# Scores of stick-breaking attention: the keys' low parts kept in 64 rows per head instead of 128

## The chip, the cores and the metric

The kernel runs on one core of a Trainium2 chip. The metric is the device time of one execution in microseconds (us), as a median of several runs. All engine times come from one execution that the hardware profiler recorded. The engines are named as the profile names them: PE (TensorE matmul), PEld (TensorE weight load), DVE (VectorE), ACT (ScalarE), POOL (GpSimd), SP (the queue that issues most DMAs).

## What is computed

One decoder layer over 1024 positions and 1024 channels in float32: a norm, one input projection, a gated short convolution beside eight heads of attention, an output projection, an MLP, a gate, a norm. The change lies in the attention. For each head of 64 channels the reference computes

```python
z = einsum('bhqd,bhkd->bhqk', q, k) * scale          # scores, 64 channels
mask = key_pos[None, :] < q_pos[:, None]
log_keep = where(mask, log_sigmoid(-z), 0.0)
suffix = cumsum(log_keep, axis=3, reverse=True) - log_keep
a = where(mask, exp(log_sigmoid(z) + suffix), 0.0)
out = einsum('bhqk,bhkd->bhqd', a, v)
```

## The kernel before

Every large product takes float32 operands apart into a high part, rounded to the matmul's format, and a low part, the rest. In the projections three matmuls are summed: high x high, high x low, low x high. ACT makes a high part (a copy), DVE the low part (a subtraction).

The scores use the fact that a head has 64 channels and a matmul sums over 128 rows. The query tile of a head holds the high parts in the 64 rows that the head owns (rows 0 to 63 for head 0 of a pair, 64 to 127 for head 1) and the low parts in the other 64. For the keys there are two tiles per head: K1 holds the high parts in both halves, K2 the low parts in both halves. Two matmuls over 128 rows then give the sum of all four products (L583).

The heads come in four pairs. `qk_projection(pr)` makes the queries and keys of a pair: for each half of the positions (512), 24 matmuls (L155) fill one bank of PSUM, ACT copies the high parts out of it (L449, L463, L464), and DVE subtracts (L450, L465, L466). L465 writes the low parts of the keys into the head's own rows, L466 into the other 64. The tiles come from a group of nine units ("QK"); a projection waits until six are free and takes two for the queries and four for the keys. A head's three units go back when its last score is issued.

`attend_front` computes scores for blocks of 128 queries: per piece of up to 512 keys one pair of matmuls (L583), two sigmoids on ACT (L585, L586), a mask on POOL (L590), running products on DVE (L593, L598), a product on POOL or DVE (L600). There are 96 such pieces. `back_transposes` turns 128x128 blocks of the result on PE (L612), ACT rounds them (L617), DVE takes the low parts (L618). `back_values` multiplies by the values (L642): the high part first, then the low part, so its second matmul waits for L618. ACT and DVE add up the halves (L650, L651). `head_norm` (L483 to L498, with a power on POOL at L494) runs in between.

On PE the order is the program's own. `attention_slots` yields slots, and between the slots the generator `fillers` hands out matmuls of the projections, the convolution branch and the output projection, 8 per slot. Between two scores PE therefore has other matmuls to do. In this stage the order on ACT, DVE, POOL and SP is set by a scheduler at build time, and each engine takes its queue strictly in that order. The stage runs from about 100 us to 454 us of the span; the MLP follows.

Of the kernel before, what the change touches and what calls it, by code (L numbers as in the profile page):

```python
# [10 lines left out]
F32R = mybir.dt.float32r  # L11
AF = mybir.ActivationFunctionType
ALU = mybir.AluOpType

P = 128
# [41 lines left out]
def f32(ap):  # L57
    return ap.bitcast(F32)
# [3 lines left out]
def hybrid_layer_kernel(ctx: ExitStack, tc: tile.TileContext, x, p, g_mix, w_in, conv_w, g_conv_out,  # L62
                        g_attn_out, w_out, g_mlp, w_up, w_down, g_ple, w_ple_gate, w_ple_proj,
                        g_final, out):
    nc = tc.nc
    x, p, w_in, conv_w, w_out, w_up, w_down, w_gate, w_proj, out = (
        x[0], p[0, 0], w_in[0], conv_w[0], w_out[0], w_up[0], w_down[0], w_ple_gate[0], w_ple_proj[0], out[0])
# [6 lines left out]
    U = Units(upool, {"A": 16, "VY": 10, "QK": 9, "T": 9, "W": 5, "C": 2, "E": 3})  # L74
    PS_BUFS = {"mm": 2, "z": 2, "tr": 2, "av": 2}

    def bank(tag):
        return psum.tile([P, HB], F32, name="ps_" + tag, tag=tag, bufs=PS_BUFS[tag])
# [309 lines left out]
    def proj_bank(ps, w2, h):  # L388
        yield from product_steps(ps, [(w2[0][0][:, d, :], w2[1][0][:, d, :], aT(h, d, 0), aT(h, d, 1))
                                      for d in range(KT)])  # L390

    class Stream:
# [17 lines left out]
        def next(self):  # L410
            self._split()
            return self.ready.popleft()
# [17 lines left out]
    QK = {}  # L430
# [1 line left out]
    normed = set()  # L432

    def qk_projection(pr):
        while len(U.free_q["QK"]) < 6:
            yield 0
        w2 = stream.next()
        Q = [U.get("QK", F32R) for _ in range(2)]
        K = [[U.get("QK", F32R) for _ in range(2)] for _ in range(2)]
        QK[pr] = (Q, K)  # L440
        for h in range(NH):
            ps = bank("mm")
            yield from proj_bank(ps, w2, h)
            sl = slice(h * HB, (h + 1) * HB)
            for hd in range(2):
                src = ps[hd * 64:hd * 64 + 64]
                hi = Q[hd][0][hd * 64:hd * 64 + 64, sl]
                lo = Q[hd][0][64 - hd * 64:128 - hd * 64, sl]
                nc.scalar.activation(hi, src, AF.Copy, scale=0.125)  # L449
                nc.vector.scalar_tensor_tensor(out=lo, in0=src, scalar=0.125, in1=f32(hi),  # L450
                                               op0=ALU.mult, op1=ALU.subtract)
        stream.done(w2)
        w2 = stream.next()
        for h in range(NH):
            ps = bank("mm")
            yield from proj_bank(ps, w2, h)
            sl = slice(h * HB, (h + 1) * HB)
            for hd in range(2):
                src = ps[hd * 64:hd * 64 + 64]
                own = slice(hd * 64, hd * 64 + 64)  # L460
                oth = slice(64 - hd * 64, 128 - hd * 64)
                K1, K2 = K[hd][0][0], K[hd][1][0]
                nc.scalar.copy(out=K1[own, sl], in_=src)  # L463
                nc.scalar.copy(out=K1[oth, sl], in_=src)  # L464
                nc.vector.tensor_tensor(out=K2[own, sl], in0=src, in1=f32(K1[own, sl]), op=ALU.subtract)  # L465
                nc.vector.tensor_tensor(out=K2[oth, sl], in0=src, in1=f32(K1[own, sl]), op=ALU.subtract)  # L466
        stream.done(w2)
        qk_ready.add(pr)

# [91 lines left out]
    def attend_front(pr, hd, c):  # L561
        Q, K = QK[pr]
        q, k1, k2 = Q[hd][0], K[hd][0][0], K[hd][1][0]
        both = c < 2
        if both:
            ku, bu = U.get("T", F32), U.get("T", F32)
        views, units = [], []
        for i, tb in enumerate((2 * c, 2 * c + 1)):
            n = P * (tb + 1)
            if both:  # L570
                keep, beta = ku[0][:, i * HB:i * HB + n], bu[0][:, i * HB:i * HB + n]
            else:
                ku, bu = U.get("T", F32), U.get("T", F32)
                keep, beta = ku[0][:, 0:n], bu[0][:, 0:n]
            views.append(beta)
            if i == 1 or not both:
                units.append(bu)
            cut = 384 if n == 640 else HB
            for s0 in ((cut, 0) if n > HB else (0,)):
                s1 = n if s0 or n <= HB else cut  # L580
                z = bank("z")
                for j, k in enumerate((k1, k2)):
                    nc.tensor.matmul(z[:, :s1 - s0], q[:, tb * P:(tb + 1) * P], k[:, s0:s1],  # L583
                                     start=(j == 0), stop=(j == 1))
                nc.scalar.activation(keep[:, s0:s1], z[:, :s1 - s0], AF.Sigmoid, scale=-1.0)  # L585
                nc.scalar.activation(beta[:, s0:s1], z[:, :s1 - s0], AF.Sigmoid)  # L586
                e = s1
                if s1 == n:
                    dg = beta[:, n - P:n]
                    nc.gpsimd.affine_select(out=dg, in_=dg, pattern=[[-1, P]], compare_op=ALU.is_gt, fill=0.0,  # L590
                                            base=0, channel_multiplier=1)
                    rev = keep[:, n - P:n][:, ::-1]
                    nc.vector.tensor_tensor_scan(out=rev, data0=rev, data1=future[:, ::-1], initial=1.0,  # L593
                                                 op0=ALU.mult, op1=ALU.max)
                    s1, e = n - P, n - 1
                if s1 > s0:
                    rev = keep[:, s0:s1][:, ::-1]
                    nc.vector.tensor_tensor_scan(out=rev, data0=rev, data1=rev, initial=keep[:, s1:s1 + 1],  # L598
                                                 op0=ALU.mult, op1=ALU.bypass)
                (nc.vector if s0 > 0 and pr < 3 else nc.gpsimd).tensor_tensor(  # L600
                    out=beta[:, s0:e], in0=beta[:, s0:e], in1=keep[:, s0 + 1:e + 1], op=ALU.mult)
                if s0 == 0 and (i == 1 or not both):
                    U.put(ku)
                yield views, units

    def back_transposes(ch, jp, narrow):
        c, views = ch["c"], ch["views"]
        tp = bank("tr")
        diag = jp == c
        blocks = [(2 * jp, 0), (2 * jp, 1)] + ([] if diag else [(2 * jp + 1, 0)]) + [(2 * jp + 1, 1)]  # L610
        for i, (j, t) in enumerate(blocks):
            nc.tensor.transpose(tp[:, i * P:(i + 1) * P], views[t][:, j * P:(j + 1) * P], ident)  # L612
            next(narrow, None)
        w = len(blocks) * P
        aT2 = U.get("T", F32R, (P, 2, HB))
        ah, al = aT2[0][:, 0, :], aT2[0][:, 1, :]
        nc.scalar.copy(out=ah[:, :w], in_=tp[:, :w])  # L617
        nc.vector.tensor_tensor(out=al[:, :w], in0=tp[:, :w], in1=f32(ah[:, :w]), op=ALU.subtract)  # L618
        if diag:
            for u in ch["units"]:  # L620
                U.put(u)
        return aT2
# [39 lines left out]
    def attention_slots():  # L662

        def fronts():
            for pr in range(4):
                while pr not in qk_ready:
                    yield -1
                for hd in range(2):  # L670
                    for c in range(4):
                        ch = {"pr": pr, "hd": hd, "c": c}
                        for views, units in attend_front(pr, hd, c):
                            ch["views"], ch["units"] = views, units
                            yield pr
                        for jp in range(c + 1):
                            backq.append((slot[0] + LAG, ch, jp))
                    Q, K = QK[pr]
                    U.put(Q[hd])
                    for u in K[hd]:  # L680
                        U.put(u)

        fr = fronts()
        live = True
        while live or backq or pend:
            slot[0] += 1
            narrow = iter(())
            while pend and pend[0][0] <= slot[0]:
                for _ in narrow:
                    pass  # L690
                narrow = back_values(*pend.popleft()[1:])
                next(narrow, None)
            if backq and backq[0][0] <= slot[0]:
                _, ch, jp = backq.popleft()
                pend.append((slot[0] + LAG_V, ch, jp, back_transposes(ch, jp, narrow)))
            for _ in narrow:
                pass
            run_deferred()
            if live and len(U.free_q["T"]) >= 3:
                live = next(fr, None) is not None  # L700
            yield
# [948 lines left out]
```

## Time and profile before

| | us |
|---|---|
| median of 3 runs (1270.54 to 1271.71) | 1270.54 |
| the profiled execution | 1272.67 |
| its span, first to last instruction | 1271.0 |
| PE busy | 1213.7 (95%) |
| DVE busy | 975.7 (77%) |
| ACT busy | 628.2 (49%) |
| POOL busy | 232.2 (18%) |

Matmuls overlap in the records: a record of 512 columns lasts about 0.4 us, while the starts lie 0.23 us apart in an undisturbed row. A busy share of 100% therefore means that PE never lacks work; what one matmul costs is read from the distances of the starts. The view of waits names the engine for which an idle engine waited. Over the whole span TensorE's granted clock was 0.987 of full speed.

### The profile page before, as it was taken

How to read it: one execution, taken by the hardware profiler on the slowest of the kernel's cores; microseconds unless marked ns; L12 is line 12 of the kernel's file. 1: busy time of each engine (PE TensorE's matmuls, PEld its weight loads, DVE VectorE, ACT ScalarE, POOL GpSimd, SP SyncE). 2: the span in 40 equal slices, each digit the busy share in tenths (PEclk: the TensorE clock that was granted, in tenths of full speed). 3: DMA queues.
4: the chain of work that ended last, by engine and by line, in shares of the span. 5: the costliest groups of instructions: out<-in, count | busy, mean ns of one | idle time of the engine just before them, and what ended most of it. 6: DMA issues, size and time to landing. Idle time of an engine off the chain costs nothing.

```text
span 1271.0 us, 15672 instructions
## 1 busy us (share of the span) xinstructions
PE 1213.7 (95%) x5629; PEld 1002.6 (79%) x5629; DVE 975.7 (77%) x1422; ACT 628.2 (49%) x1049; POOL 232.2 (18%) x248
## 2 busy tenths in 40 slices
PE   8999999999998899899999999987999999999997
PEld 6788878878877688678888888865788888887786
DVE  3656898999989986777666766656889888877774
ACT  4445465555656442456555555462344444445543
POOL 2402443535448540100000000000000000002121
PEclk8999999999999999999999999998999999999999
DMA  9711101111122315324577677789887886667432
GB/s 360 220 34 41 36 25 34 34 34 34 34 67 83 116 51 201 113 91 156 203 282 260 245 283 259 266 287 322 256 258 230 255 260 200 203 202 226 138 100 100
DMA packets 152229, 209.71 MB, mean 165 GB/s; under 512 B 8004, under 2 KB 111448, under 8 KB 152152
## 3 DMA queue, kind: packets, MB, share of 16 engines
q1 hardware_dynamic: 151608, 207.67, 48.7%
q8 instruction: 44, 0.72, 0.2%
q10 hardware_dynamic: 544, 1.05, 0.2%
q14 instruction: 33, 0.27, 0.1%
HBM read 141.58 MB, written 67.11 MB: 164 GB/s over the span
## 4 chain that ended last, share of the span: by engine, by line
PE 50%; DMA 4%; DVE 4%; ACT 1%; issue 1%; SPq 0%; POOL 0%; DVEq 0%; POOLq 0%; ACTq 0%
PE ps_z L1013 12%; PE ps_mm L1013 12%; PE ps_av L1013 12%; PE ps_tr L1013 7%; DMA u<-h_d 2%; PE ps_z L155 2%; PE ps_tr L155 2%; PE ps_mm L155 2%; PE ps_av L155 2%; DVE u L905 1%; DVE u L1276 1%; DVE u L836 1%; DMA n_d<-u 1%; DMA u<-hs_d 1%; DVE u L839 1%
## 5 line engine op out<-in xcount | busy, mean ns | idle before, releaser
L155 PE MATMUL ps_mm<-u,u 128*128 128x512 f32 (+1 forms) x1464 | 366.5, 396 | 7.7 <-ACT u L901 2.8
L155 PEld LDWEIGHTS ps_mm<-u,u 128*128 128x128 f32 x1464 | 270.1, 190 | 62.6 <-ACT u L901 3.2
L905 DVE TENSOR_TENSOR u<-u,u 128x1024 fp32r<-128x1024 f32 (+2 forms) x214 | 231.0, 1099 | 42.4 <-ACT u L901 35.2
L901 ACT CAST u<-u 128x1024 fp32r<-128x1024 f32 (+2 forms) x214 | 195.1, 952 | 90.4 <-DVE u L839 20.4
L1013 PE MATMUL ps_z<-u,u 128*128 128x512 f32 x768 | 195.9, 398 | 14.0 <-DVE u L905 6.7
L1013 PE MATMUL ps_mm<-u,u 128*128 128x512 f32 x768 | 191.9, 392 | 5.0 <-DVE u L836 4.4
L1013 PE MATMUL ps_av<-u,u 128*128 128x512 f32 x744 | 185.6, 391 | 2.0 <-DVE u L905 1.4
L1013 PEld LDWEIGHTS ps_z<-u,u 128*128 128x128 f32 x768 | 146.5, 192 | 47.9 <-DVE u L905 8.3
L1013 PEld LDWEIGHTS ps_mm<-u,u 128*128 128x128 f32 x768 | 145.2, 189 | 36.6 <-DVE u L836 5.3
L1013 PEld LDWEIGHTS ps_av<-u,u 128*128 128x128 f32 x744 | 140.0, 188 | 32.6 <-DVE u L905 2.1
L120 POOL TENSOR_SCALAR me<-ms 128x1 f32<-128x1 f32 x24 | 10.3, 431 | 704.7 <-DVE u L836 618.0
L836 DVE TENSOR_TENSOR u<-ps_av,u 128x512 f32<-128x512 f32 x94 | 64.6, 688 | 80.6 <-PE ps_av L1013 47.7
L1013 PE MATMUL ps_tr<-u,u 128*128 128x512 f32 x408 | 100.4, 389 | 0.0
L600 POOL TENSOR_TENSOR u<-u,u 128x383 f32<-128x383 f32 (+5 forms) x72 | 72.5, 1009 | 110.5 <-DVE u L598 70.9
L1013 PEld LDWEIGHTS ps_tr<-u,u 128*128 128x128 f32 x408 | 76.5, 188 | 15.9
L839 DVE TENSOR_TENSOR u<-u,u 128x512 f32<-128x512 f32 (+1 forms) x120 | 84.2, 723 | 1.7
L598 DVE TENSOR_TENSOR_SCAN u<-u 128x128 f32<-128x128 f32 (+3 forms) x88 | 83.7, 951 | 2.3 <-ACT u L585 0.3
L617 ACT CAST u<-ps_tr 128x512 fp32r<-128x512 f32 (+1 forms) x80 | 43.4, 543 | 58.3 <-PE ps_tr L612 57.7
L642 PEld LDWEIGHTS ps_av<-u,u 128*128 128x128 f32 x320 | 50.1, 189 | 24.7 <-DVE u L618 17.9
L642 PE MATMUL ps_av<-u,u 128*128 128x256 f32 (+1 forms) x320 | 54.8, 284 | 13.6 <-DVE u L618 13.2
L110 ACT CAST u<-u 128x1024 fp32r<-128x1024 f32 x42 | 43.9, 1055 | 29.1 <-DVE u L498 10.4
L494 POOL TENSOR_TENSOR hrs<-hms,mhalf 128x16 f32<-128x16 f32 x16 | 52.7, 3296 | 28.8 <-DVE hms L492 28.7
(132 smaller groups left out, 1502.7 us busy)
## 6 DMA issues: line engine op xcount, KB each, us to landing
u<-in_w_down SPq DMA_DIRECT2D x56, 512.0 KB, 5.4
u<-hs_d SPq DMA_DIRECT2D x64, 448.0 KB, 5.8
hs_d<-u SPq DMA_DIRECT2D x48, 512.0 KB, 2.8
u<-in_w_up SPq DMA_DIRECT2D x32, 512.0 KB, 6.0
ws_d<-u SPq DMA_DIRECT2D x32, 512.0 KB, 2.8
u<-ws_d SPq DMA_DIRECT2D x32, 512.0 KB, 6.4
u<-in_w_in SPq DMA_DIRECT2D x24, 512.0 KB, 4.2
u<-in_x SPq DMA_DIRECT2D x16, 512.0 KB, 8.1
```

The costliest lines, as they stand in the source:

```text
L110: nc.scalar.copy(out=hi, in_=raw)
L155: nc.tensor.matmul(ps, a, b, start=(i == 0), stop=(i == n - 1))
L494: nc.gpsimd.tensor_tensor(out=rs, in0=ms, in1=mhalf, op=ALU.pow)
L598: nc.vector.tensor_tensor_scan(out=rev, data0=rev, data1=rev, initial=keep[:, s1:s1 + 1], op0=ALU.mult, op1=ALU.bypass)
L600: (nc.vector if s0 > 0 and pr < 3 else nc.gpsimd).tensor_tensor(out=beta[:, s0:e], in0=beta[:, s0:e], in1=keep[:, s0 + 1:e + 1], op=ALU.mult)
L617: nc.scalar.copy(out=ah[:, :w], in_=tp[:, :w])
L642: nc.tensor.matmul(av[:, t0:256], v, part[:, c0:c0 + 256 - t0], start=(j == 0 and part is ah), stop=(j == n - 1 and part is al))
L836: (eng or nc.vector).tensor_tensor(out=out, in0=a, in1=b, op=ALU.add)
L839: (eng or nc.vector).tensor_tensor(out=out, in0=a, in1=b, op=ALU.subtract)
L901: nc.scalar.copy(out=box["o"][0], in_=src())
L905: nc.vector.tensor_tensor(out=b, in0=src(), in1=f32(a), op=ALU.subtract)
L1013: nc.tensor.matmul(ps, a, b, start=(fresh and i == 0), stop=(i == n - 1), skip_group_check=not fresh)
```

## The change

The low parts of the keys are written once, into the head's own 64 rows. So both heads of a pair share one unit for them, and L466 goes away: 16 subtractions of 64x512, in each of the four pairs one per head and half. The second matmul of a score now takes 64 rows of the query tile, the high parts, and the 64 rows of low key parts. The product of low and low is no longer in the sum. A projection of queries and keys takes five units instead of six.

```diff
 def qk_projection(pr):
-    while len(U.free_q["QK"]) < 6:
+    while len(U.free_q["QK"]) < 5:
         yield 0
     w2 = stream.next()
     Q = [U.get("QK", F32R) for _ in range(2)]
-    K = [[U.get("QK", F32R) for _ in range(2)] for _ in range(2)]
+    KL = U.get("QK", F32R)
+    K = [[U.get("QK", F32R), KL] for _ in range(2)]
...
             nc.scalar.copy(out=K1[own, sl], in_=src)
             nc.scalar.copy(out=K1[oth, sl], in_=src)
             nc.vector.tensor_tensor(out=K2[own, sl], in0=src, in1=f32(K1[own, sl]), op=ALU.subtract)
-            nc.vector.tensor_tensor(out=K2[oth, sl], in0=src, in1=f32(K1[own, sl]), op=ALU.subtract)
...
             z = bank("z")
-            for j, k in enumerate((k1, k2)):
-                nc.tensor.matmul(z[:, :s1 - s0], q[:, tb * P:(tb + 1) * P], k[:, s0:s1],
-                                 start=(j == 0), stop=(j == 1))
+            own = slice(hd * 64, hd * 64 + 64)
+            nc.tensor.matmul(z[:, :s1 - s0], q[:, tb * P:(tb + 1) * P], k1[:, s0:s1], start=True, stop=False)
+            nc.tensor.matmul(z[:, :s1 - s0], q[own, tb * P:(tb + 1) * P], k2[own, s0:s1], start=False, stop=True)
...
         U.put(Q[hd])
-        for u in K[hd]:
-            U.put(u)
+        U.put(K[hd][0])
+        if hd == 1:
+            U.put(K[hd][1])
```

The scheduler gives ACT, DVE, POOL and SP a slightly other order. On DVE, in the projection of the third pair (in the trace about 267 to 275 us), the rows before are these. The names are tiles; the number behind u_ tells units apart; order prints the running products of L598 as SCALAR_TENSOR_TENSOR.

```order
L465 TENSOR_TENSOR u_2273<-ps_mm,u_2272 64x512
L600 TENSOR_TENSOR u_2526<-u_2526,u_2525 128x511
L466 TENSOR_TENSOR u_2273<-ps_mm,u_2272 64x512
L618 TENSOR_TENSOR u_2547<-ps_tr,u_2547 128x512
L465 TENSOR_TENSOR u_2275<-ps_mm,u_2274 64x512
L466 TENSOR_TENSOR u_2275<-ps_mm,u_2274 64x512
L497 STREAM_TRANSPOSE u_2485<-hrs 128x512
L618 TENSOR_TENSOR u_2577<-ps_tr,u_2577 128x384
L598 SCALAR_TENSOR_TENSOR u_2525<-u_2525 128x512
L498 SCALAR_TENSOR_TENSOR u_1962<-u_1962,gc,u_2485 128x512
```

The same place on DVE in the changed kernel, where the subtraction of L465 stands in line 466:

```order
L466 TENSOR_TENSOR u_2262<-ps_mm,u_2263 64x512
L600 TENSOR_TENSOR u_2515<-u_2515,u_2514 128x511
L618 TENSOR_TENSOR u_2536<-ps_tr,u_2536 128x512
L466 TENSOR_TENSOR u_2262<-ps_mm,u_2264 64x512
L618 TENSOR_TENSOR u_2564<-ps_tr,u_2564 128x384
L598 SCALAR_TENSOR_TENSOR u_2514<-u_2514 128x512
L497 STREAM_TRANSPOSE u_2474<-hrs 128x512
L498 SCALAR_TENSOR_TENSOR u_1952<-u_1952,gc,u_2474 128x512
```

Both copies of L466 are gone, and the transposition of L497 has moved behind the second L618 and the running product of L598. The projection of the fourth pair changes in the same way.

On PE nothing moves; every matmul stands where it stood. Around a score of the first pair the rows before are these (u_824 and u_825 are K1 and K2 of head 0, u_822 its queries, L155 a projection that fills in):

```order
L155 MATMUL ps_mm<-u_211,u_886 128x512
L155 MATMUL ps_mm<-u_215,u_886 128x512
L155 MATMUL ps_mm<-u_211,u_887 128x512
L583 MATMUL ps_z<-u_824,u_822 128x256
L583 MATMUL ps_z<-u_825,u_822 128x256
L155 MATMUL ps_mm<-u_211,u_886 128x512
```

And in the changed kernel (u_825 is now K1, u_824 the shared tile of low parts):

```order
L155 MATMUL ps_mm<-u_211,u_885 128x512
L155 MATMUL ps_mm<-u_215,u_885 128x512
L155 MATMUL ps_mm<-u_211,u_886 128x512
L583 MATMUL ps_z<-u_825,u_822 128x256
L584 MATMUL ps_z<-u_824,u_822 128x256
L155 MATMUL ps_mm<-u_211,u_885 128x512
```

Only the second matmul of the score differs: it has its own line, and it reads 64 rows where its neighbours on both sides read 128.

## Rows read from the trace of the kernel before

**Rows 1.** Stretches, scores of L583 alone: length, PE busy (matmuls), PEld busy (loads), clock, DMA.

```profile
100.00:116.40 16.40, 1.85 (x8) 1.50 (x8) 1.00 0.22 65
116.40:181.30 64.90, 11.02 (x38) 5.84 (x38) 1.00 0.11 33
181.30:274.20 92.90, 14.55 (x50) 7.69 (x50) 1.00 0.10 29
274.20:359.00 84.80, 13.99 (x48) 7.28 (x48) 1.00 0.14 44
359.00:401.20 42.20, 7.59 (x28) 4.20 (x28) 1.00 0.17 57
401.20:454.00 52.80, 6.44 (x22) 3.08 (x21) 0.97 0.32 111
```

**Rows 2.** PE's waits, first four stretches (us, times, longest); the fifth reads as the second.

```profile
PE ps_mm L155 <- DVE u L466: 0.4, 1, 0.4
...
PE ps_av L642 <- DVE u L618: 1.7, 1, 1.7
...
PE ps_av L642 <- DVE u L618: 2.7, 3, 1.2
...
PE ps_av L642 <- DVE u L618: 2.6, 3, 1.2
```

**Rows 3.** The last stretch, all work: PE, PEld, DVE, ACT, POOL busy.

```profile
401.20:454.00 52.80, 45.65 (x226) 36.33 (x226) 52.03 (x78) 26.34 (x49) 33.26 (x28) 0.97 0.32 111
```

**Rows 4.** DVE by line, the whole span: count, busy us, mean ns, idle before.

```profile
L466 DVE TENSOR_TENSOR u<-ps_mm,u 64x512 fp32r<-64x512 f32 x16 | 11.0, 689 | 0.2
```

**Rows 5.** Timeline of DVE in the third pair's projection: start, us, instruction.

```profile
268.82 0.69 DVE L466 TENSOR_TENSOR u<-ps_mm,u 64x512 fp32r<-64x512 f32 x1
269.54 0.69 DVE L618 TENSOR_TENSOR u<-ps_tr,u 128x512 fp32r<-128x512 f32 x1
...
271.46 0.69 DVE L466 TENSOR_TENSOR u<-ps_mm,u 64x512 fp32r<-64x512 f32 x1
272.18 0.71 DVE L497 STREAM_TRANSPOSE u<-hrs 128x512 f32<-128x512 f32 x1
272.92 0.56 DVE L618 TENSOR_TENSOR u<-ps_tr,u 128x384 fp32r<-128x384 f32 x1
```

**Rows 6.** Timeline of ACT at that place, with its idle time and whom it awaited.

```profile
269.54 0.58 ACT L463 CAST u<-ps_mm 64x512 fp32r<-64x512 f32 x1 [3.69 <-DVE u L466]
```

**Rows 7.** Timeline of PE at that place.

```profile
270.29 0.62 PE L642 MATMUL ps_av<-u,u 128*128 128x256 f32 x3 [1.19 <-DVE u L618]
...
273.54 0.56 PE L642 MATMUL ps_av<-u,u 128*128 128x256 f32 x3 [1.14 <-DVE u L618]
```

**Rows 8.** Timeline of PE, and of its weight loads, around L105, which has 20 rows.

```profile
24.06 0.84 PE L155 MATMUL ps_mm<-u,u 128*128 128x512 f32 x3
24.84 0.23 PE L105 MATMUL ps_tr<-ident,u 20*128 20x20 f32 x1
25.00 0.38 PE L135 MATMUL ps_tr<-ident,u 128*128 128x128 f32 x1
...
25.45 1.30 PE L155 MATMUL ps_mm<-u,u 128*128 128x512 f32 x5
...
24.83 0.13 PEld L105 LDWEIGHTS ps_tr<-ident,u 20*128 20x128 f32 x1 [0.35 <-issue]
```

**Rows 9.** Timeline of PE where nothing disturbs it, with a score.

```profile
302.18 2.23 PE L155 MATMUL ps_mm<-u,u 128*128 128x512 f32 x9
304.25 0.60 PE L612 MATMUL ps_tr<-ident,u 128*128 128x128 f32 x4
304.60 0.71 PE L583 MATMUL ps_z<-u,u 128*128 128x512 f32 x2
305.15 0.40 PE L155 MATMUL ps_mm<-u,u 128*128 128x512 f32 x1
```

## The prediction, made before the changed kernel ran

> **What bounds the kernel now.** I read the page's busy shares first, then the waits of PE and the busy time in the attention stage (100 to 454 us), because both edits lie there, and last the timelines at the two places where they act. PE leads them and DVE follows, so a microsecond counts if it is PE's own work or a wait of PE. The stage holds 96 score pairs, 192 matmuls. I cut it where PE waits, into six stretches; by the counts of [rows 1] they hold 4, 19, 25, 24, 14 and 10 pairs (the pair at 401 us touches two stretches and is counted in the fifth). In the first five PE waits 0.4, 1.7, 2.7, 2.6 and 1.7 us for DVE [rows 2], 9.1 us together: nearly always the second value matmul (L642), which needs the low part from L618. In the last stretch DVE is busy 52.03 of 52.80 us and PE 45.65 [rows 3]; there DVE sets the time, and PE has some 7 us to spare. So PE has little slack in the stage and DVE, beside it, hardly more.
>
> **What the change removes.** L466 goes: 16 subtractions of 689 ns, 11.0 us of DVE [rows 4]. Most of it is off the path, since DVE idles or catches up elsewhere. It counts where PE waits behind it:
> - First stretch: PE waits 0.4 us for an L466 itself [rows 2], since the subtraction is the last reader of the projection's bank. That wait ends.
> - Third pair's projection: L618 at 269.54 stands right behind an L466 at 268.82 [rows 5], and PE's wait of 1.19 us ends with it [rows 7]. Without L466 it starts 0.7 us sooner. The next wait, 1.14 us, is for the L618 at 272.92, which stands behind another L466 and behind L497; the changed order puts L497 after it. ACT's copy for head 1 at 269.54 had idled 3.69 us for an L466 [rows 6]; it too starts earlier. This second wait can vanish. Together 0.7 + 1.14 = 1.8 us.
> - Fourth pair's projection: the same pattern, waits of the same size (three, longest 1.2, sum 2.6) [rows 2], so another 1.8 us.
> - Second pair's projection and the fifth stretch: the waits of 1.7 us stand before the second pair's L466 and well after the fourth pair's last ones. No gain.
>
> Sum of the gain, if nothing else changed: 0.4 + 1.8 + 1.8 = 4.0 us. The unit saved changes no wait: five units are free at the same moment as six were, when head 0 of the pair before is done. On PE no instruction moves. On SP one load of x goes ahead of two loads of w_out, which come long before their use; on ACT and POOL a few neighbours swap. I cost these at nothing, because none of them ends a wait in [rows 2]; if one did, it would be by one instruction, well under 1 us.
>
> **What the change adds.** The second matmul of a pair runs as many columns as before, so it streams no faster, and weight loads are already hidden: nine matmuls of 512 columns start within 304.25 - 302.18 = 2.07 us, 0.23 us each [rows 9]. A gain on PE is therefore excluded. What is new is that each of the 96 pairs goes from 128 rows to 64 and back. The trace has one instruction over fewer rows, the 20-row transposition of L105. Three matmuls from 24.06 should have let it start 0.69 us later; it started 0.78 us later, at 24.84 [rows 8]: 0.09 us late, and its weight load, idle before, waited for nothing that the profile shows ("issue"). The whole detour, from 24.06 to the matmul at 25.45, took 1.39 us. At the undisturbed pace it would be four matmuls, 4 x 0.23 = 0.92, and two transpositions. Four transpositions and two scores take 305.15 - 304.25 = 0.90 us [rows 9], less 2 x 0.23 leaves 0.44, so 0.11 each: 0.92 + 0.22 = 1.14. The detour cost 0.25 us. Part of that may be the semaphore by which L135 waits for L105. So per pair:
> - at least 0, if a 64-row matmul behaves like a 128-row one;
> - 0.09, if only the entry costs;
> - 0.18, if entry and return cost 0.09 each;
> - 0.25, as the detour shows;
> - at most 0.34: one record lasts 0.40 us where starts are 0.23 apart [rows 9], so 0.17 us of overlap is there to lose, twice.
>
> I take 0.25, the only measured round trip; the ends stay in the range.
>
> The Trainium skill, "TensorEngine Tiling (Array Packing)", section "Key Properties", says that changing the tiling mode, unlike the tile alone, makes TensorE drain. This case's 0.09 us before L105 agrees in sign. It gives no price; the skill's "TensorE: Matmul & The Clock Gate", section "Single matmul latency", puts the drain at about 175 ns, from which 96 x 2 x 0.175 = 33.6 us would be an estimate before any of it is absorbed, against 24.0 us by the row.
>
> **What lies beside other work.** A later PE meets DVE's results without waiting, so a stretch grows only by what exceeds its wait. With a price s per pair the five stretches grow by 4s - 0.4, 19s - 1.7, 25s - 2.7, 24s - 2.6 and 14s - 1.7. In the last, 10s = 2.5 us goes into the 7 us that PE has to spare. At s = 0.25: 0.6 + 3.05 + 3.55 + 3.4 + 1.8 = 12.4 us (86s - 9.1). That the waits can vanish whole rests on DVE not being later itself; in the third and fourth stretches the removed L466 make room, in the second and fifth it is an assumption. Without any of it the cost would be 24 us, less the gain of 4.0.
>
> **The sum.** Profiled execution: 1272.67 + 12.4 = 1285.1 us. That execution stands 2.1 us above the median of the runs, so for the median 1270.54 + 12.4 = **1282.9 us**. With s between 0.18 and 0.34 the formula gives +6.4 to +20.1, the forecast's own range 1276.9 to 1290.6.
>
> **Rival 1: the change of rows costs nothing (faster).** Then only the removed subtractions count: 4.0 us less, 1266.5. Place: the waits at 270.29 and 273.54 and their twins in the fourth pair. For it: the rows show exactly these subtractions ahead of the awaited L618; the late L105 is one instruction, a transposition, ahead of which other waits were resolved. Against it: the 0.09 us that no wait explains. By the formula the sign turns at s = 9.1 / 86 = 0.11 us; below that this rival decides.
>
> **Rival 2: only the entry costs, 0.09 us (no change).** PE gets 96 x 0.09 = 8.6 us more work, and the waits take it up: 86 x 0.09 - 9.1 = -1.4 us, 1269.2. For it: the clean part of the detour is just this. Against it: the return at L135 was late too.
>
> Differences under 0.2% (2.5 us) are about what a measurement of this kernel cannot tell from no change.
>
> **How the numbers follow.** Forecast 0.60, rival 1 0.26, rival 2 0.14. The range takes in both rivals and the upper bound of the price, 1265.5 to 1291; left out are a price above the bound and a DVE that absorbs nothing. Faster by over 0.2%: nine tenths of rival 1, and a little of rival 2: 0.24. Within 0.2%: most of rival 2, the rest of rival 1, the forecast's lowest edge: 0.15. Slower: 0.61.
>
> **What would show it.** In the profile after: DVE 11.0 us less busy; in undisturbed places the start of L584 later than 0.23 us after L583 for 512 columns, and the matmul after L584 late again, 0.25 us together per pair (this settles forecast against rivals at once); the waits for L618 in the third and fourth stretches gone; the last stretch about as long as before. The forecast is wrong if the starts keep 0.23 us, or if the waits stay while the matmuls slow down.

## The result

The changed kernel takes 1293.76 us (median of 3 runs, 1292.42 to 1294.85) against 1270.54 us before. The ratio is 1.0175, with a 95% interval of 1.0153 to 1.0198. It is slower, as forecast, by 23.2 us where 12.4 were forecast, and 2.8 us above the upper end of the range.

The page of the profile after, span 1290.7 us:

```profile
PE 1245.1 (96%) x5629; PEld 1006.4 (78%) x5629; DVE 966.0 (75%) x1406; ACT 631.5 (49%) x1049; POOL 230.2 (18%) x248
```

DVE has 16 instructions fewer, and its busy time fell from 975.7 to 966.0 us. PE has the same 5629 instructions and is busy 31.4 us longer. What takes longer is seen at one score, in the timeline of PE after (start, duration, instruction):

```profile
307.64 0.38 PE L612 MATMUL ps_tr<-ident,u 128*128 128x128 f32 x2
307.78 0.47 PE L583 MATMUL ps_z<-u,u 128*128 128x512 f32 x1
308.18 0.50 PE L584 MATMUL ps_z<-u,u 64*128 64x512 f32 x1
308.61 0.96 PE L155 MATMUL ps_mm<-u,u 128*128 128x512 f32 x3
...
308.95 0.62 PE L155 MATMUL ps_mm<-u,u 128*128 128x512 f32 x2
```

The last row is the second of the three L155 in the row above it. Before, [rows 9], a score behind transpositions took 305.15 - 304.60 = 0.55 us from its first start to the next instruction's, and the L155 after that 0.23. Now it is 308.61 - 307.78 = 0.83 and 308.95 - 308.61 = 0.34. That is 0.28 + 0.11 = 0.39 us more for one score. The weight loads at the same place show where it goes:

```profile
307.75 0.19 PEld L583 LDWEIGHTS ps_z<-u,u 128*128 128x128 f32 x1
308.18 0.18 PEld L584 LDWEIGHTS ps_z<-u,u 64*128 64x128 f32 x1 [0.24 <-issue]
308.61 0.30 PEld L155 LDWEIGHTS ps_mm<-u,u 128*128 128x128 f32 x2 [0.25 <-issue]
```

In an undisturbed row each load starts with the matmul ahead of it and is over before that ends. Here the load for the 64-row matmul starts only at 308.18, together with its own matmul's record, 0.24 us after the last load ended, and waits for nothing that the profile shows. On the way back the load of L155 does the same at 308.61. It is the pattern of L105 in [rows 8], twice per score.

The waits of PE in the attention stage (100 to 490 us; us, times, longest) before, 16.6 us together:

```profile
PE ps_av L642 <- DVE u L618: 13.2, 12, 1.7
PE ps_tr L612 <- POOL u L600: 1.4, 3, 0.7
PE ps_mm L155 <- DVE u L111: 1.0, 1, 1.0
PE ps_mm L155 <- DVE u L466: 0.4, 1, 0.4
PE ps_av L642 <- ACT u L617: 0.3, 1, 0.3
PE ps_mm L155 <- DVE u L722: 0.3, 1, 0.3
```

And after:

```profile
PE ps_av L642 <- DVE u L618: 3.5, 2, 2.1
PE ps_tr L612 <- POOL u L600: 1.3, 1, 1.3
```

Only 4.8 us are left. The stage, from the first score to the last value matmul, is read from two rows of each kernel (count; shortest, median and longest duration in ns; first and last start in us). Before:

```profile
L642 PE MATMUL ps_av<-u,u x320: 221/281/389, 122.2 to 464.3; 128*128 128x256 f32 x128, 128*128 128x128 f32 x32
L583 PE MATMUL ps_z<-u,u x192: 220/365/478, 108.3 to 444.9; 128*128 128x512 f32 x80, 128*128 128x256 f32 x48, 128*128 128x384 f32 x48, 128*128 128x128 f32 x16
```

After:

```profile
L642 PE MATMUL ps_av<-u,u x320: 221/282/579, 121.4 to 484.1; 128*128 128x256 f32 x128, 128*128 128x128 f32 x32
L583 PE MATMUL ps_z<-u,u x96: 220/385/775, 105.9 to 465.0; 128*128 128x512 f32 x40, 128*128 128x256 f32 x24, 128*128 128x384 f32 x24, 128*128 128x128 f32 x8
```

464.3 - 108.3 = 356.0 us before, 484.1 - 105.9 = 378.2 after: 22.2 us longer, although PE waits 16.6 - 4.8 = 11.8 us less. By this reckoning PE's own work grew by 34.0 us, or 0.35 us for each of the 96 scores.

That is less than the starts give, because the list counts a wait only from the end of the last record, and a record outlasts the pace. One wait of the kernel before, and the same place after:

```profile
178.68 0.32 PE L642 MATMUL ps_av<-u,u 128*128 128x256 f32 x1
180.69 0.62 PE L642 MATMUL ps_av<-u,u 128*128 128x256 f32 x3 [1.69 <-DVE u L618]
...
184.56 0.64 PE L642 MATMUL ps_av<-u,u 128*128 128x256 f32 x4
185.03 0.49 PE L612 MATMUL ps_tr<-ident,u 128*128 128x128 f32 x3
```

Listed with 1.69 us, the wait put 180.69 - 178.68 = 2.01 us between two starts. After, four starts take 185.03 - 184.56 = 0.47 us, 0.12 each: 1.89 us less. PE's order is the same in both kernels, so all starts can be compared one by one. From the matmul ahead of a score to the third behind it the distance grows by 0.37 to 0.41 us at 85 of the 96 scores, by 0.28 to 0.30 at the eight of 128 columns; at the other three a wait or a lower clock falls in. That is 0.39 us in the median and 36.9 us in all. The rest of the stage became 14.7 us shorter, which leaves the 22.2.

The last ten scores, which lie in the last stretch of [rows 1], took their share too. This L155 stands behind the 86th score, before and after:

```profile
401.31 0.63 PE L155 MATMUL ps_mm<-u,u 128*128 128x512 f32 x1
...
418.75 0.50 PE L155 MATMUL ps_mm<-u,u 128*128 128x512 f32 x1
```

From it to the last value matmul it is 464.3 - 401.31 = 63.0 us before and 484.1 - 418.75 = 65.4 after, 2.4 more; the other 19.8 of the 22.2 lie ahead of it. In this part TensorE's granted clock fell to about half of full speed (1.2 GHz), for 3.4 us before and for 10.2 after; the later fall came after PE had waited 2.1 us for L618. The rows give length, busy time of PE, PEld, DVE, ACT and POOL, clock and DMA:

```profile
401.30:404.70 3.40, 3.40 (x10) 2.65 (x9) 3.40 (x3) 0.93 (x3) 2.25 (x2) 0.51 0.51 152
...
431.50:441.70 10.20, 8.79 (x24) 6.23 (x24) 9.28 (x13) 2.23 (x5) 5.04 (x4) 0.50 0.81 296
```

How much of the 2.4 us this accounts for, no run separates. From the last value matmul to the end it is 806.7 us before and 806.6 after; nothing changed there. The span of the profiled executions differs by only 19.7 us because in the one after the first score came 2.4 us earlier, a difference that lies before the stage.

### The profile page after: what moved, and what is told of

Read it like the earlier page. It is cut to its first block, busy times and chain, and to the rows that moved or that the text cites. A ratio compares the mean times of both kernels' runs of the same rounds, so it can differ in the third digit from the quotient of the medians.

```text
span 1290.7 us, 15653 instructions
## 1 busy us (share of the span) xinstructions
PE 1245.1 (96%) x5629; PEld 1006.4 (78%) x5629; DVE 966.0 (75%) x1406; ACT 631.5 (49%) x1049; POOL 230.2 (18%) x248
## 4 chain that ended last, share of the span: by engine, by line
PE 49%; DMA 4%; DVE 4%; ACT 1%; issue 1%; SPq 0%; POOL 0%; DVEq 0%; POOLq 0%; ACTq 0%
PE ps_z L1014 12%; PE ps_mm L1014 12%; PE ps_av L1014 12%; PE ps_tr L1014 6%; DMA u<-h_d 2%; PE ps_z L155 2%; PE ps_tr L155 2%; PE ps_mm L155 2%; PE ps_av L155 1%; DVE u L1277 1%; DVE u L837 1%; DVE u L906 1%; DMA n_d<-u 1%; DMA u<-hs_d 1%; DVE u L840 1%
## 5 line engine op out<-in xcount | busy, mean ns | idle before, releaser
L155 PE MATMUL ps_mm<-u,u 128*128 128x512 f32 (+1 forms) x1464 | 374.8, 401 | 6.6 <-ACT u L902 3.1
L155 PEld LDWEIGHTS ps_mm<-u,u 128*128 128x128 f32 x1464 | 264.2, 189 | 75.7 <-issue 14.5
L1014 PEld LDWEIGHTS ps_mm<-u,u 128*128 128x128 f32 x768 | 145.7, 190 | 36.8 <-DVE u L837 5.5
L598 DVE TENSOR_TENSOR_SCAN u<-u 128x128 f32<-128x128 f32 (+3 forms) x88 | 84.7, 962 | 4.8 <-ACT u L585 2.7
L600 POOL TENSOR_TENSOR u<-u,u 128x383 f32<-128x383 f32 (+5 forms) x72 | 69.2, 962 | 94.1 <-DVE u L598 59.9
L618 DVE TENSOR_TENSOR u<-ps_tr,u 128x512 fp32r<-128x512 f32 (+1 forms) x80 | 50.5, 632 | 27.2 <-ACT u L617 26.3
L585 ACT ACTIVATE u<-ps_z 128x384 f32<-128x384 f32 (+3 forms) x96 | 47.4, 494 | 28.2 <-PE ps_z L584 26.4
```

The costliest lines, as they stand in the source:

```text
L155: nc.tensor.matmul(ps, a, b, start=(i == 0), stop=(i == n - 1))
L1014: nc.tensor.matmul(ps, a, b, start=(fresh and i == 0), stop=(i == n - 1), skip_group_check=not fresh)
```

## The experiments

Four of the six kernels ran beside the kernel before on one chip (median 1270.78 us), the two with doubled matmuls on another occasion (1271.45 us).

**The shared tile without the change of rows.** In the changed kernel the second matmul takes all rows again (the output slice of z, which is the same in every kernel, is shortened here and below):

```diff
-nc.tensor.matmul(z[...], q[own, tb * P:(tb + 1) * P], k2[own, s0:s1], start=False, stop=True)
+nc.tensor.matmul(z[...], q[:, tb * P:(tb + 1) * P], k2[:, s0:s1], start=False, stop=True)
```

> The changed kernel, but the second matmul of each score runs over all 128 rows of the query tile and of the shared tile of low key parts. It leaves the right sum: the other 64 rows add this head's low query parts times the other head's low key parts. All else is as changed: no second copy of the low parts, five units, the new order on DVE, ACT, POOL, SP. Theory A (going from 128 to 64 rows and back costs PE about 0.40 us per score, as the starts in the trace after show): the cost is gone and the gain on DVE is left, 1270.5 - 4.0 = 1266.5 us. Rival B (the shared tile, the five units or the new order make it slow): about 1294 us, as the changed kernel.

Measured: 1265.93 us, ratio 0.995 (0.9933 to 0.9966). With 128 rows the same tiles, units and orders are 4.9 us faster than before. Rival B falls: nothing in the shared tile or in the moved instructions makes the changed kernel slow. The gain is where the prediction put it, in the first, third and fourth stretches. Timeline of DVE, then of PE, in the third pair's projection of this kernel:

```profile
266.26 0.68 DVE L466 TENSOR_TENSOR u<-ps_mm,u 64x512 fp32r<-64x512 f32 x1
266.87 0.67 DVE L600 TENSOR_TENSOR u<-u,u 128x511 f32<-128x511 f32 x1
267.46 0.68 DVE L618 TENSOR_TENSOR u<-ps_tr,u 128x512 fp32r<-128x512 f32 x1
268.19 0.69 DVE L466 TENSOR_TENSOR u<-ps_mm,u 64x512 fp32r<-64x512 f32 x1
268.91 0.56 DVE L618 TENSOR_TENSOR u<-ps_tr,u 128x384 fp32r<-128x384 f32 x1
```

```profile
268.19 0.62 PE L642 MATMUL ps_av<-u,u 128*128 128x256 f32 x3 [0.39 <-DVE u L618]
268.65 1.53 PE L155 MATMUL ps_mm<-u,u 128*128 128x512 f32 x6
270.02 0.57 PE L642 MATMUL ps_av<-u,u 128*128 128x256 f32 x4
```

The wait of 1.19 us [rows 7] is 0.39 us here, and the wait of 1.14 us is gone: the second L618 follows 0.7 us after the only subtraction ahead of it, where two subtractions and L497 stood [rows 5].

**The 64 rows without the rest.** The kernel before, with both copies of the low parts, and the score of the changed kernel:

```diff
-for j, k in enumerate((k1, k2)):
-    nc.tensor.matmul(z[...], q[:, tb * P:(tb + 1) * P], k[:, s0:s1], start=(j == 0), stop=(j == 1))
+nc.tensor.matmul(z[...], q[:, tb * P:(tb + 1) * P], k1[:, s0:s1], start=True, stop=False)
+nc.tensor.matmul(z[...], q[own, tb * P:(tb + 1) * P], k2[own, s0:s1], start=False, stop=True)
```

> The kernel before with one edit: the second matmul of each score takes 64 rows; both copies of the low parts are still written, six units. Theory A: the price of 0.40 us per score, 38 us on PE, less what PE's waits take up, and without the gain on DVE: 1293 to 1298 us. Rival B: 1270.5 us, as before.

Measured: 1293.0 us, ratio 1.0167 (1.0151 to 1.0182). It is at the lower edge of what was expected, and this one edit carries the whole loss. In the total the 16 subtractions, worth 4.9 us where PE keeps its pace, are worth nothing that can be measured once PE is slower: with them 1293.0, without them 1293.76, two intervals that overlap. Its stage and waits:

```profile
L642 PE MATMUL ps_av<-u,u x320: 221/282/387, 123.9 to 485.4; 128*128 128x256 f32 x128, 128*128 128x128 f32 x32
L583 PE MATMUL ps_z<-u,u x96: 220/385/481, 108.4 to 465.6; 128*128 128x512 f32 x40, 128*128 128x256 f32 x24, 128*128 128x384 f32 x24, 128*128 128x128 f32 x8
```

```profile
PE ps_tr L612 <- POOL u L600: 2.0, 2, 1.7
PE ps_av L642 <- DVE u L618: 2.0, 3, 1.4
PE ps_mm L155 <- DVE u L111: 0.6, 1, 0.6
```

485.4 - 108.4 = 377.0 us, 21.0 more than before, with 12.0 us less waiting: 33.0 us of PE, 0.34 per score by the list of waits; by the starts it is 0.39 in the median here too.

The traces show where the gain went. The L155 behind the 86th score, and the clock after it, in this kernel:

```profile
422.87 0.50 PE L155 MATMUL ps_mm<-u,u 128*128 128x512 f32 x1
...
428.60:432.00 3.40, 3.40 (x12) 2.72 (x11) 3.32 (x5) 2.49 (x5) 3.40 (x3) 0.50 0.37 128
```

Up to there the stage has 422.87 - 108.4 = 314.5 us, in the changed kernel 418.75 - 105.9 = 312.9, so 1.6 us of the gain are left. Behind it this kernel has 485.4 - 422.87 = 62.5 us and the changed one 65.4, where the clock was at half for 10.2 us instead of 3.4. With one trace of each, it stays open whether the lower clock is what took the gain back.

**Half of the scores.** Head 0 of a pair in 64 rows, head 1 in 128:

```diff
+rows = own if hd == 0 else slice(0, P)
-nc.tensor.matmul(z[...], q[own, tb * P:(tb + 1) * P], k2[own, s0:s1], start=False, stop=True)
+nc.tensor.matmul(z[...], q[rows, tb * P:(tb + 1) * P], k2[rows, s0:s1], start=False, stop=True)
```

> The changed kernel, where only head 0 of each pair (rows 0 to 63) has its second matmul over 64 rows; head 1 runs it over 128 rows of the shared tile, which adds a wrong term. 48 scores change rows instead of 96. Theory A: half the PE cost, 19 us, less the waits that take it up: about 1277 us (1273 to 1282). Rival D (the price hangs on which 64 rows, a tile that does not begin at row 0): 1266.5 us.

Measured: 1279.92 us, ratio 1.0066 (1.0045 to 1.0088), 9.1 us slower. Between no change of rows (4.9 us faster) and 96 changes (23.2 slower) the middle is 9.2. The price counts by scores, and rows 0 to 63 pay it as well. Rival D falls.

**Two 64-row matmuls in a row, and two of 128 rows.** The second matmul is issued twice, once in the changed kernel, once in the first experiment's:

```diff
+for last in (False, True):
-nc.tensor.matmul(z[...], q[own, tb * P:(tb + 1) * P], k2[own, s0:s1], start=False, stop=True)
+    nc.tensor.matmul(z[...], q[own, tb * P:(tb + 1) * P], k2[own, s0:s1], start=False, stop=last)
```

> The changed kernel with the 64-row matmul of each score issued twice in a row (the product with the low key parts is added twice, which is not the reference). Theory A1 (the price belongs to the change between 128 and 64 rows): the second 64-row matmul starts 0.23 us after the first for 512 columns, and only its columns are added, 96 scores of 384 columns on average at 0.17 us: 16 us, about 1310 us. Rival E (every matmul over 64 rows pays, whatever stands ahead of it, since its weights cannot be loaded under another): it starts some 0.4 us after the first, and 35 us are added, about 1328 us.

> The same doubling in the kernel whose second matmul runs over 128 rows of the shared tile (its wrong term is added twice): the measure for one more matmul where rows do not change. 16 us more on PE, of which the waits for DVE that are left take up a part: theory A1 and rival E both say 1266 + 7 to 16 us, 1273 to 1282 us, and starts 0.23 us apart.

Measured: 1309.44 us, ratio 1.0302 (1.0264 to 1.0339), and 1278.34 us, ratio 1.0058 (1.0038 to 1.0078). Against the same kernels without the doubling that is 15.7 and 12.4 us (these two ran on other occasions, on which the kernel before took 0.7 and 0.9 us less). A second 64-row matmul costs its columns and no second 0.39 us; rival E falls by its time, 1328 us. One number of the expectation missed: the two 64-row matmuls do not start 0.23 us apart (the two of 128 rows do). The timeline of PE with two 64-row matmuls:

```profile
320.06 0.47 PE L583 MATMUL ps_z<-u,u 128*128 128x512 f32 x1
320.46 0.73 PE L585 MATMUL ps_z<-u,u 64*128 64x512 f32 x2
...
320.80 0.39 PE L585 MATMUL ps_z<-u,u 64*128 64x512 f32 x1
321.12 1.20 PE L155 MATMUL ps_mm<-u,u 128*128 128x512 f32 x4
```

The second starts 0.34 us after the first, and L155 0.32 after that. Taken alone, 0.34 lies nearer to rival E's 0.4 than to 0.23; the whole way from L583 to L155 decides, 321.12 - 320.06 = 1.06 us against 0.83 with one 64-row matmul, which is one pace of 0.23 more. In the changed kernel L155 came 0.43 us after the only one. So the 0.20 us above the pace of 0.23 splits in two: 0.11 follows the entry (the first 64-row matmul's weights are loaded in the open) and 0.09 comes ahead of the return (nothing starts, and the load of L155 has not begun). A change of rows costs about 0.2 us each way: 0.09 before the load, 0.11 for the load.

**Low x low left out, all rows kept.** If the change of rows is the price, the layout can be turned so that no matmul changes rows. The keys get one tile per head, high parts in the own rows and low parts in the others; the queries get two, the high parts in both halves, and the low parts beside zeros:

```diff
+for hd in range(2):
+    nc.gpsimd.memset(f32(Q[hd][1][0][64 - hd * 64:128 - hd * 64]), 0.0)
...
-hi = Q[hd][0][hd * 64:hd * 64 + 64, sl]
-lo = Q[hd][0][64 - hd * 64:128 - hd * 64, sl]
-nc.scalar.activation(hi, src, AF.Copy, scale=0.125)
-nc.vector.scalar_tensor_tensor(out=lo, in0=src, scalar=0.125, in1=f32(hi), op0=ALU.mult, op1=ALU.subtract)
+nc.scalar.activation(Q1[own, sl], src, AF.Copy, scale=0.125)
+nc.scalar.activation(Q1[oth, sl], src, AF.Copy, scale=0.125)
+nc.vector.scalar_tensor_tensor(out=Q2[own, sl], in0=src, scalar=0.125, in1=f32(Q1[own, sl]), op0=ALU.mult, op1=ALU.subtract)
...
-nc.scalar.copy(out=K1[own, sl], in_=src)
-nc.scalar.copy(out=K1[oth, sl], in_=src)
-nc.vector.tensor_tensor(out=K2[own, sl], in0=src, in1=f32(K1[own, sl]), op=ALU.subtract)
-nc.vector.tensor_tensor(out=K2[oth, sl], in0=src, in1=f32(K1[own, sl]), op=ALU.subtract)
+nc.scalar.copy(out=KH[own, sl], in_=src)
+nc.vector.tensor_tensor(out=KH[oth, sl], in0=src, in1=f32(KH[own, sl]), op=ALU.subtract)
...
-for j, k in enumerate((k1, k2)):
+for j, q in enumerate((q1, q2)):
     nc.tensor.matmul(z[...], q[:, tb * P:(tb + 1) * P], k[:, s0:s1], start=(j == 0), stop=(j == 1))
```

> Without low x low, but with every matmul over 128 rows: per head one key tile (high parts in the own 64 rows, low parts in the others) and two query tiles, the high parts in both halves, and the low parts in the own half with zeros in the other, which POOL writes. Six units. Against before DVE has 16 subtractions of 64x512 fewer, ACT as many copies, POOL eight fills of 64x1024 more. Theory A: the gain on DVE without the price on PE, 1264 to 1269 us. Rival B would put it down to the tile and unit changes, and says nothing of this layout. Rival C (the subtractions removed stand on no path): 1270.5 us, within 0.2%.

Measured: 1265.68 us, ratio 0.9957 (0.9944 to 0.997). This version is faster than both kernels, by 5.1 us and 28.1 us. The sums are those of the changed kernel. Rival C falls: without the second copies the time is below 1270.5 us. The fills that POOL adds do not show in the time, which is that of the first experiment; their group in the view by line (busy us, mean ns, idle before):

```profile
L441 POOL MEMSET u<- 64x1024 f32 x8 | 7.6, 951 | 0.3
```

## Why the prediction was right or wrong

- **What bounds the stage**: right. PE took the added work into its time, and its waits shrank from 16.6 to 4.8 us, those for DVE from 14.9 to 3.5.
- **The gain on DVE**, 4.0 us by three places: right, and measured alone at 4.9 us (first experiment). Compared start by start, that kernel's first, third and fourth stretches are 0.7, 3.4 and 2.4 us shorter than before and its last 1.1 longer, so the places are right and the 1.8 for the third and the fourth is too small. The two kernels without the second copies that keep 128 rows agree, 1265.9 and 1265.7 us. That a gain on DVE and a loss on PE do not simply add was in the formula, and the second experiment shows it: with the loss in place the total has no gain.
- **The sign and the mechanism of the loss**, the change between 128 and 64 rows: right, and isolated by the first two experiments from either side.
- **The price per score**: wrong, and this is the step that failed. The term s was taken as 0.25 us from the detour at L105; the starts after give 0.39, at the quoted score and in the median, above the upper bound of 0.34. The entry was read well: 0.09 us of [rows 8] is the 0.09 of every entry. What was missed is the load in the open, 0.11 us after either change. It was in [rows 8] too, but I subtracted it: I priced L105 at 0.11, the pace of 128-column transpositions, whereas L105 has 20 columns. At 20/128 of that pace, 0.02, the same detour costs 1.39 - 0.92 - 0.11 - 0.02 = 0.34 us, for which the formula gives 1290.6. Where the remaining 0.05 lies is argued only: L105's load is shorter as well, 0.13 us [rows 8] against 0.18 for 64 rows. And the bound of 0.34 counted the lost overlap of two records, which is not a bound on a load that cannot be hidden. The estimate of 33.6 us set beside the sum lies nearer to the 36.9 measured than the 24.0 by the row, but its term, 0.175 us each way for the drain alone, is not what the starts show: 0.09 without a start and 0.11 of a load.
- **What lies beside other work**: right in direction; that its size comes out near is in part luck. With 0.35 for s the formula gives 86 x 0.35 - 9.1 = 21.0 us, but 0.35 comes from the stage and the listed waits themselves, so this tests nothing. With 0.39 it gives 24.4 for the first five stretches. They grew by 19.8, and the last stretch, whose share was to vanish in PE's slack, by 2.4. The waits gave back more than the 9.1 us listed (1.89 for one listed with 1.69), and the removed subtractions some 1.6. The two misses offset each other in part, and the stage grew by 22.2, the median by 23.2.
- **The check announced**, the distances around L584, settled forecast against rivals: L584 starts late, and so does the matmul after it. Of the other signs, DVE is 9.7 us less busy where 11.0 was said, the waits for L618 in the third and fourth stretches are gone, and the last stretch, said to stay about as long, is 2.4 us longer. Rival 1 (1266.5 us) is the first experiment's time, which means that its price would have been right without the change of rows. Rival 2 needs a return without cost; the return costs as much as the entry.

## What to carry to other kernels

A matmul that sums over half of the rows saves no time on PE if its neighbours sum over all of them; put zeros or another useful product into the free rows, or set matmuls of one row count next to each other, since two in a row paid one entry and one return here. When an operand can be halved on either side, look which side lets the matmuls keep their shape. And price a shape that hardly stands in the trace by every start behind it until the old pace is back, not by the first late one.

## What the runs showed of the hardware

- Going from 128 to 64 rows and back costs PE 0.39 us per visit (0.37 to 0.41 at 85 of 96 scores): each way about 0.09 us in which nothing starts and about 0.11 us for a weight load that is otherwise hidden.
- The scores of 256, 384 and 512 columns pay the same 0.39 us, those of 128 columns 0.28 to 0.30. At one of only 128 columns in the changed kernel, in the timeline of PE, the distances are 0.23 and 0.26 us:

```profile
375.71 0.30 PE L583 MATMUL ps_z<-u,u 128*128 128x128 f32 x1
375.94 0.32 PE L584 MATMUL ps_z<-u,u 64*128 64x128 f32 x1
376.20 2.32 PE L155 MATMUL ps_mm<-u,u 128*128 128x512 f32 x9
```

In the first experiment, with 128 rows, such a score has 0.15 and 0.11 us, together 0.23 less (the rest lies in the next start):

```profile
272.91 0.30 PE L583 MATMUL ps_z<-u,u 128*128 128x128 f32 x1
273.06 0.28 PE L584 MATMUL ps_z<-u,u 128*128 128x128 f32 x1
273.17 2.31 PE L155 MATMUL ps_mm<-u,u 128*128 128x512 f32 x9
```

- The profile does not name it. The busy share of PE hardly moved (95% to 96%), no wait is listed, and the gap stands only before the weight loads, as "issue".
